# All 32 hidden rows of the MLP down projection by seven products, with half 0's norm rows beneath the last two stages

## The chip, the cores and the metric

One core of a Trainium2 chip runs the whole program. The metric is the time of one execution on the device in microseconds (us): the median of several runs of the kernel before is 2182.65. TensorE multiplies matrices, ScalarE (ACT in the profile) and VectorE (DVE) work on tiles of 128 partitions, SyncE (SP) issues loads, and ScalarE also issues stores.

## The reference

A trunk of two layers over 1024 rows of 1024 features. Layer 0 has a short convolution, layer 1 latent attention whose keys and values are made once from the stream after layer 0. Each layer ends with an MLP of 4096 hidden features. What the change touches is the MLP's second product and the norm and residual behind it:

```python
def squared_relu_mlp(h, w_up, w_down):
    return jnp.square(jax.nn.relu(h @ w_up)) @ w_down
...
        y = squared_relu_mlp(h, mlp_up_w[l], mlp_down_w[l])
        x = x + g_f[:, None, :] * rmsnorm(y, norm_g[l, 3])
```

In layer 0 the new x is normed again (without its gains, which are folded into later scales), turned into columns and multiplied by the latent weights `q_a_w` and `kv_a_w`. In layer 1 it is the output. All of it is in float32.

## The kernel before

Every float32 operand is split into a high and a low part (`split_w`: ScalarE writes the high part, L160, VectorE subtracts it for the low part, L161), and a product is three matmuls, high by low, low by high, high by high (`mm`, L157). A step of the down projection is thus a row of splits that ScalarE and VectorE must have finished, and then matmuls.

The hidden activations are 32 rows of 128 features, in DRAM, transposed: `ha`, seven sums of quarters for pairs of rows, and `hd`, plain rows. `down_pairs` takes 24 of the 32 rows as 12 pairs, and multiplies 2 x 2 blocks in the seven-product way of Strassen and Winograd: seven stages in the order 0, 1, 3, 6, 4, 5, 2, six steps each. A stage accumulates in four PSUM banks, one for each row tile t; a pair of stages that share a result go on in the same banks. A step loads its operand `raw<-ha` through four buffers (`raw_tile`), splits it into a ring buffer `pa` (three of them), splits its quarter of the weight, which stays in its own room `w`, into a ring buffer `pb` (two), and runs 24 matmuls. After a stage, `sums`, `add` or `copy` bring the banks into the eight result tiles `ys`, rows 128 t to 128 t + 127. Half 0 is tiles 0 to 3, half 1 tiles 4 to 7.

`down` then does the other 8 rows directly in chunks of 2, 2 and 4. In its last chunk `Seam.tile` follows for each of the eight row tiles: it adds the last bank, takes squares and root on ScalarE (L246, L248), scales (L303), adds the residual row (L304) and stores it; in layer 0 it takes the squares again, and `flush` writes the normed row into the result tile (L286). `first_block` makes the first three latents of half 0 with the transposes of half 1 between.

The order on each engine is fixed when the program is built: a scheduler moves instructions, but inside `pinned` those of the named engines (SP's alone where none is named) keep the order in which they are written. SP issues loads in order, and where one of them waits for a buffer, all behind it wait. The lines that matter here are few:

```python
    def ld(out_, in_):
        nc.sync.dma_start(out_, in_)
...
                nc.vector.tensor_tensor(xr, xr, y, op=ALU.add)
                nc.scalar.dma_start(self.xdst[t * P:(t + 1) * P, :], xr)
```

## Time and profile before

| | before |
|---|---|
| three runs, us | 2182.33, 2182.65, 2184.46 |
| profiled execution, us | 2181.45 |
| its span, us | 2179.7 |
| granted TensorE clock, mean | 0.992 |
| TensorE, VectorE, ScalarE busy | 96%, 70%, 48% |
| layer 0: products; direct rows; first latents, us | 716 to 955; to 1044; to 1070 |
| layer 1: direct rows to the end, us | 2083 to 2180 |

A row of the timeline has the start, the duration, the engine, the line, the operation and its tiles; in square brackets is the idle time before it and what ended that. TensorE's matmuls overlap, so what counts is the distance between starts. Groups have the count, then busy time and mean nanoseconds, then the idle time before them. Numbers of buffers are left out of names: `ring` is any of the ring buffers, `raw` any buffer of loads.

### The profile page before, as it was taken

The numbers are of one execution on the slowest core, as the hardware profiler recorded it, in microseconds if no ns is written. First come the engines' busy times: TensorE is split into PE (matmuls) and PEld (weight loads), VectorE is DVE, ScalarE is ACT, GpSimd is POOL, SyncE is SP. The second block draws the span as 40 slices with busy tenths as digits, with TensorE's granted clock in tenths as the row PEclk, the third lists the DMA queues.
The fourth block names the chain that finished last, engine by engine and source line by source line (L and its number), as shares of the span: only waits on it lengthen the run. The fifth ranks groups of instructions, "written<-read, shape, count | busy, mean of one in ns | idle before, by whom it ended". The sixth has DMA issues, their size and how long they took to land.

```text
span 2179.7 us, 25250 instructions
## 1 busy us (share of the span) xinstructions
PE 2093.7 (96%) x9638; PEld 1715.7 (79%) x9638; DVE 1530.3 (70%) x2063; ACT 1052.2 (48%) x1501; POOL 4.0 (0%) x8
## 2 busy tenths in 40 slices
PE   4999999899999999999899999999899999999998
PEld 3778888678888788888777888877688887788886
DVE  6777766876665679766788887666866655566665
ACT  4533354744454444343665655565645544444422
POOL 0000000000000000000000000000000000000000
PEclk9999999999999999999999999999999999999999
DMA  7435464256443986554223231053254544842343
GB/s 226 131 119 154 128 203 144 78 164 193 160 159 104 342 292 199 162 168 147 85 66 122 69 113 44 30 185 115 81 164 156 179 160 153 295 174 97 127 134 116
DMA packets 233552, 323.52 MB, mean 148 GB/s; under 512 B 18165, under 2 KB 141394, under 8 KB 233430
## 3 DMA queue, kind: packets, MB, share of 16 engines
q1 hardware_dynamic: 198424, 244.11, 35.7%
q10 hardware_dynamic: 35006, 77.79, 9.3%
q8 instruction: 76, 1.25, 0.2%
q14 instruction: 46, 0.38, 0.1%
HBM read 244.26 MB, written 77.59 MB: 148 GB/s over the span
## 4 chain that ended last, share of the span: by engine, by line
PE 79%; DVE 11%; ACT 6%; issue 2%; DMA 1%; ACTq 0%; SPq 0%; DVEq 0%
PE one L157 39%; PE mm L157 19%; PE big L157 9%; PE tp L157 6%; PE big L1280 2%; ACT junk L246 2%; DVE y L303 2%; DVE raw L304 2%; PE tp L1306 1%; DVE y L297 1%; ACT z L1137 1%; DMA aw<-in_ada_w_dram 1%; ACT small L248 1%; DVE av L823 1%; PE tp L399 0%
## 5 line engine op out<-in xcount | busy, mean ns | idle before, releaser
L157 PE MATMUL one<-slot,uphi 128*128 128x512 f32 x1224 | 378.3, 390 | 0.0
L157 PE MATMUL big<-slot 128*128 128x512 f32 x1536 | 354.3, 391 | 0.6 <-DVE slot L161 0.6
L157 PEld LDWEIGHTS big<-slot 128*128 128x128 f32 x1536 | 288.5, 188 | 60.5 <-DVE slot L161 0.8
L157 PEld LDWEIGHTS one<-slot,uphi 128*128 128x128 f32 x1224 | 230.8, 189 | 48.3 <-issue 0.5
L157 PE MATMUL one<-slot,uplo 128*128 128x512 f32 x612 | 241.0, 394 | 8.1 <-ACT y L565 2.3
L161 DVE TENSOR_TENSOR uplo<-raw,uphi 128x1024 fp32r<-128x1024 f32 x127 | 153.2, 1221 | 131.6 <-ACT uphi L160 131.5
L157 PE MATMUL one<-ring,ring 128*128 128x512 f32 x864 | 198.2, 390 | 2.8 <-DVE ring L161 2.8
L160 ACT ACTIVATE ring<-w 128x1024 fp32r<-128x1024 f32 x84 | 88.9, 1059 | 224.0 <-PE tp L157 117.5
L160 ACT ACTIVATE uphi<-raw 128x1024 fp32r<-128x1024 f32 x127 | 134.5, 1061 | 121.6 <-PE one L157 89.4
L157 PEld LDWEIGHTS one<-ring,ring 128*128 128x128 f32 x864 | 161.7, 188 | 38.3 <-ACT ring L160 3.1
L157 PE MATMUL mm<-slot,uphi 128*128 128x512 f32 x520 | 164.2, 396 | 9.7 <-DVE slot L364 9.3
L161 DVE TENSOR_TENSOR ring<-w,ring 128x1024 fp32r<-128x1024 f32 x84 | 102.7, 1223 | 89.0 <-ACT ring L160 86.7
L157 PEld LDWEIGHTS one<-slot,uplo 128*128 128x128 f32 x612 | 115.4, 189 | 35.7 <-ACT y L490 3.3
L157 PE MATMUL mm<-ring,ring 128*128 128x512 f32 x576 | 139.5, 390 | 0.1
L157 PE MATMUL tp<-ring,ring 128*128 128x512 f32 x576 | 138.7, 389 | 0.0
L187 DVE SCALAR_TENSOR_TENSOR acc<-raw,csil,acc 128x1024 f32<-128x1024 f32 x88 | 112.5, 1279 | 32.3 <-DMA raw<-in_ada_w_dram 29.2
L157 PEld LDWEIGHTS mm<-ring,ring 128*128 128x128 f32 x576 | 107.6, 188 | 23.5 <-issue 0.8
L157 PEld LDWEIGHTS tp<-ring,ring 128*128 128x128 f32 x576 | 108.1, 188 | 22.4
L157 PEld LDWEIGHTS mm<-slot,uphi 128*128 128x128 f32 x520 | 97.2, 189 | 33.2 <-DVE slot L364 10.8
L490 ACT ACTIVATE y<-one 128x512 f32<-128x512 f32 x66 | 39.0, 591 | 165.8 <-PE one L157 95.7
L157 PE MATMUL one<-slot,s 128*128 128x512 f32 x468 | 112.6, 389 | 0.0
L161 DVE TENSOR_TENSOR ring<-raw,ring 128x1024 fp32r<-128x1024 f32 x84 | 102.4, 1219 | 11.9 <-ACT ring L160 11.9
(252 smaller groups left out, 3495.9 us busy)
## 6 DMA issues: line engine op xcount, KB each, us to landing
ha<-y ACTq DMA_DIRECT2D x168, 256.0 KB, 4.0
raw<-ha SPq DMA_DIRECT2D x84, 512.0 KB, 4.3
raw<-in_ada_w_dram SPq DMA_DIRECT2D x80, 512.0 KB, 4.2
raw<-in_mlp_up_w_dram SPq DMA_DIRECT2D x70, 512.0 KB, 4.2
w<-in_mlp_down_w_dram SPq DMA_DIRECT2D x48, 512.0 KB, 6.7
raw<-hd SPq DMA_DIRECT2D x32, 512.0 KB, 4.3
hd<-y ACTq DMA_DIRECT2D x24, 512.0 KB, 3.6
xs<-raw ACTq DMA_DIRECT2D x24, 512.0 KB, 2.9
```

The costliest lines, as they stand in the source:

```text
L157: nc.tensor.matmul(out_, lhs[a], rhs[b], start=first and i == 0, stop=last and i == 2, skip_group_check=more)
L160: nc.scalar.activation(hi, src, AF.Copy)
L161: nc.vector.tensor_tensor(lo, src, hi.bitcast(F32), op=ALU.subtract)
L187: nc.vector.scalar_tensor_tensor(acc, raw, s, acc, op0=ALU.mult, op1=ALU.add)
L246: nc.scalar.activation(junk, src, AF.Square, accum_out=ss)
L248: nc.scalar.activation(rt, ss, AF.Sqrt, bias=eps_d)
L297: nc.vector.tensor_tensor(y, y, p_, op=ALU.add)
L303: nc.vector.scalar_tensor_tensor(y, y, rroot(ss), self.gmb, op0=ALU.mult, op1=ALU.mult)
L304: nc.vector.tensor_tensor(xr, xr, y, op=ALU.add)
L490: nc.scalar.activation(dst, x_, AF.Copy)
L823: nc.vector.scalar_tensor_tensor(acc, raw[:, i, :], csil[:, i:i + 1], acc, op0=ALU.mult, op1=ALU.add)
L1280: nc.tensor.matmul(o_, a, m_, start=j == 0, stop=j == 4)
```

## The change

All 32 rows now go through `down_pairs`, as 16 pairs, eight steps per stage. `down` no longer has a share in the MLP. The rings are four `pa` and three `pb`, with a fourth in the last stage, "2". The weight quarter "21" has no room of its own any more: it is loaded through the four raw buffers, in stage "1" and again in stage "2". In `mlp_up`, the first four pairs of rows make their seven quarter sums too, in place of two plain stores.

Half 0's results are complete after the fifth stage ("4"). Its four norm rows are now run beneath the last two stages, "5" and "2": tiles 0, 1 and 2 at the first, fourth and seventh step of stage "5", tile 3 at the second step of stage "2" (`half0`). Their residual rows go into tiles of their own, `xr` for odd t and `acc` for even t, one buffer each; `early` loads the residual of tile t + 2 behind the step after tile t's row. In layer 0 the transposes and evictions of half 0's columns (`h_steps`, now with two evictions by ScalarE and no VectorE copy) follow from the fourth step of stage "2" on. The last four steps of stage "2" (`LATE`) are taken by row tiles: for each t the matmuls of the four steps, and then the norm row of tile 4 + t. `first_latents` makes the first three latents one after the other, with half 1's transposes in the third. The build also sets the size of a DMA scratch area to 256.

SP's loads in layer 1 at the start of stage "5", before (`ha_110` is that stage's operand):

```order
L115 DMA raw_15651<-ha_110 128x2x512
L115 DMA raw_15682<-ha_110 128x2x512
L115 DMA raw_15713<-ha_110 128x2x512
L115 DMA raw_15744<-ha_110 128x2x512
L115 DMA raw_15775<-ha_110 128x2x512
L115 DMA raw_15806<-ha_110 128x2x512
```

And after, from the same place (`xs_104` holds the residual rows):

```order
L115 DMA xr_16020<-xs_104 128x1024
L115 DMA xr_16022<-xs_104 128x1024
L115 DMA raw_16025<-ha_110 128x2x512
L115 DMA raw_16066<-ha_110 128x2x512
L115 DMA xr_16072<-xs_104 128x1024
L115 DMA raw_16099<-ha_110 128x2x512
L115 DMA raw_16130<-ha_110 128x2x512
L115 DMA raw_16171<-ha_110 128x2x512
L115 DMA xr_16177<-xs_104 128x1024
```

The operands stood one behind the other; now two residual rows stand ahead of the first, a third between the second and the third, a fourth behind the fifth.

ScalarE in layer 0, after, in stage "5" (`y_5364` and `y_5365` are the results of tiles 0 and 1, `xr_6886` tile 0's residual; `w_5403` to `w_5406` are the weights of the second to the fifth step; `ring_5389` serves the second and the fifth):

```order
L160 ACTIVATE ring_5389<-w_5403 128x1024
L246 ACTIVATE junk_6897,small_6898<-y_5364 128x1024
L248 ACTIVATE small_6900<-small_6898,eps_d 128x1
L160 ACTIVATE ring_5385<-w_5404 128x1024
L160 ACTIVATE ring_5387<-w_5405 128x1024
L304 DMA xs_103<-xr_6886 128x1024
L246 ACTIVATE junk_6907,small_6908<-xr_6886 128x1024
L160 ACTIVATE ring_5389<-w_5406 128x1024
L248 ACTIVATE small_6910<-small_6908,eps_d 128x1
L246 ACTIVATE junk_7010,small_7011<-y_5365 128x1024
L286 ACTIVATE y_5364<-xr_6886,small_6943 128x1024
L248 ACTIVATE small_7013<-small_7011,eps_d 128x1
```

The splits stood alone there; the norm of two row tiles now stands among them, and tile 0's last write (L286) behind the split for the fifth step.

ScalarE in layer 0, after, at the end of stage "2" (`h` and `tt` are half 0's columns, `raw` operands and weights of the last steps):

```order
L160 ACTIVATE ring_5386<-raw_7408 128x1024
L398 ACTIVATE h_1001_7210<-one_7379,v_6226,v_5924 128x512
L398 ACTIVATE tt_7384<-one_7379,v_6226,v_5924 128x512
L398 ACTIVATE h_1001_7210<-one_7397,v_6226,v_5924 128x512
L398 ACTIVATE tt_7402<-one_7397,v_6226,v_5924 128x512
L398 ACTIVATE h_1001_7210<-one_7415,v_6226,v_5924 128x512
L398 ACTIVATE tt_7420<-one_7415,v_6226,v_5924 128x512
L160 ACTIVATE ring_5388<-raw_7426 128x1024
L160 ACTIVATE ring_5389<-raw_7423 128x1024
L398 ACTIVATE h_1001_7210<-one_7433,v_6226,v_5924 128x512
L398 ACTIVATE tt_7438<-one_7433,v_6226,v_5924 128x512
L160 ACTIVATE ring_5390<-raw_7444 128x1024
```

Six evictions of transposed columns stand ahead of the splits into `ring_5388` and `ring_5389`, those of the seventh step; two more ahead of the eighth's.

The diff, without the pool layout, the removed `first_block` and the calls of the attention phase:

```diff
-ROWS = 8
 LAG = 2
-PAIRS = (D_FF // P - ROWS) // 2
+PAIRS = D_FF // P // 2
+LATE = 4
...
             y = self.ys[t]
-            if t == 0:
-                self.load(0)
-                self.load(1)
-            self.load(t + 2)
+            for i in range(t, t + self.ahead):
+                self.load(i)
             xr = self.xr[t]
             with pinned():
-                nc.vector.tensor_tensor(y, y, p_, op=ALU.add)
+                if add:
+                    add()
                 self.back()
...
-    def h_steps(tp, ys, half, key, dst):
+    def h_steps(tp, ys, half, key, dst, room=tp_ps, twice=False):
         hi, lo = dst
         s1, sh = vtile["s" + key], vtile["h" + key]
         tts = {}
         def step(k):
-            p_ = tp_ps()
+            p_ = room()
             for t in range(4):
                 nc.tensor.transpose(p_[:, t * P:(t + 1) * P], ys[half * 4 + t][:, k * P:(k + 1) * P], ident)
             tt = tp.tile([P, HALF], F32, tag="tt", name=nm("tt"), bufs=2)
-            nc.scalar.activation(tt, p_, AF.Identity, scale=s1[:, k:k + 1], bias=sh[:, k:k + 1])
+            for out_ in (hi[:, k, :], tt) if twice else (tt,):
+                nc.scalar.activation(out_, p_, AF.Identity, scale=s1[:, k:k + 1], bias=sh[:, k:k + 1])
             tts[k] = tt
         def split(k):
-            nc.vector.tensor_copy(hi[:, k, :], tts[k])
+            if not twice:
+                nc.vector.tensor_copy(hi[:, k, :], tts[k])
             nc.vector.tensor_tensor(lo[:, k, :], tts[k], hi[:, k, :].bitcast(F32), op=ALU.subtract)
...
-                elif k == 1:
-                    seam.back()
-                elif k >= 4:
-                    seam.back()
-                    seam.front(steps1, 2)
+                    if m == 0 and k == 0:
+                        seam.flush()
+                    elif m == 2:
+                        seam.back()
+                        seam.front(steps, 1)
+            ps_.append(p_)
         with pinned():
             seam.back()
         return ps_
...
-    def down_pairs(ys, wd, before):
+    def down_pairs(ys, wd, before, seam, key=None, preps=()):
+        r1, r2, r3, l1 = pool("r1", "right"), pool("r2", "right"), pool("r3", "right"), pool("l1")
         n = PAIRS // 2
-        w4 = wd[ROWS * P:, :].rearrange("(q two p) d -> p q two d", two=2, p=P)
-        sl = pool("sl")
-        ws = [{} for _ in range(n)]
...
+        def room(q, b, order):
+            for i in order:
+                ws[b][i] = q.tile([P, 2, HALF], F32, name=nm("w"))
+        def ring(q):
+            return q.tile([P, 2, 2, HALF], F32R, name=nm("ring"))
+        rings = [ring(r1) for _ in range(7)]
+        room(r2, "22", range(n))
+        room(r3, "11", [5, 6, 7, 0, 1, 2, 3, 4])
+        room(l1, "12", range(n))
+        pas, pbs = rings[0::2], rings[1::2]
         count = 0
-        def get(i, b):
-            ld(ws[i][b], w4[:, 2 * i:2 * i + 2, int(b[0]) - 1, (int(b[1]) - 1) * HALF:int(b[1]) * HALF])
-        def less(i, b, x_, y_):
-            nc.vector.tensor_tensor(ws[i][b], ws[i][x_], ws[i][y_], op=ALU.subtract)
+        steps = []
...
             nc.vector.tensor_tensor(u, u, p_, op=ALU.add)
             for half in range(2):
                 nc.vector.tensor_tensor(spot(half, t, 1), spot(half, t, 1), u, op=ALU.add)
+        def products(p_, t, pa, pb, first, last, more):
+            ts_ = slice(t * P, (t + 1) * P)
+            for q in range(2):
+                mm(p_, (pa[:, 0, q, ts_], pa[:, 1, q, ts_]), (pb[:, 0, q], pb[:, 1, q]), first and q == 0, last and q == 1, more)
+        def early(t):
+            q, tag = (xp, "xr") if t % 2 else (ad, "acc")
+            seam.load(t, q.tile([P, D], F32, tag=tag, name=nm("xr"), bufs=1))
+        def half0(i):
+            if i in (0, 3, 6, n + 1):
+                seam.ahead = 1
+                seam.tile((0, 3, 6, n + 1).index(i), None, [])
+            with pinned():
+                if i in (1, 4, 7, n + 2):
+                    seam.flush()
+                    early((1, 4, 7, n + 2).index(i) + 2)
+                if i > n + 2:
+                    seam.back()
+                    seam.front(steps, 1)
+            if i in (n, n + 2, n + 7) and preps:
+                preps.pop(0)(up)
         with pinned([mybir.EngineType.SP]):
             for which, one, more, b, make, done in (
...
                 if not more:
                     banks_ = [bank_ps() for _ in range(4)] if one else [mm_ps(), mm_ps(), tp_ps(), tp_ps()]
                     spare[0] = mm_ps if one else bank_ps
-                if which == 2:
-                    sl.release()
-                    arb = pool("arB")
-                    first = slots_of(arb, SLOTS - 4)
+                late = []
+                if which == 5:
+                    l1.release()
+                    xp = pool("xp")
+                    early(0)
+                    early(1)
+                elif which == 2:
+                    r3.release()
+                    r4 = pool("r4", "right")
+                    pbs.append(ring(r4))
+                    if key:
+                        h0 = pool("h0")
+                        dst = tuple(h0.tile([P, KD, HALF], F32R, name=nm("h0")) for _ in range(2))
+                        up = pool("up")
+                        steps = h_steps(tp, ys, 0, key, dst, bank_ps, True)
                 for i in range(n):
-                    if which in (0, 1, 3, 6):
-                        get(i, b)
+                    wb = ws[b][i] if b != "21" else raw_tile().rearrange("p (q m) -> p q m", q=2)
+                    if which in (0, 1, 3, 6, 2):
+                        get(wb, i, b)
                     if make == "t3":
-                        less(i, "11", "22", "11")
+                        less(wb, ws["22"][i], wb)
                     elif make:
-                        less(i, b, b, make)
+                        less(wb, wb, ws[make][i])
                     raw = raw_tile().rearrange("p (q m) -> p q m", q=2)
                     ld(raw, ha[which][2 * i:2 * i + 2].rearrange("q p m -> p q m"))
-                    pa, pb = pas[count % 3], pbs[count % 2]
+                    m = len(pbs)
+                    pa, pb = pas[count % 4], pbs[i % 4 if m == 4 else count % 3]
                     count += 1
                     with pinned([mybir.EngineType.Activation, mybir.EngineType.DVE]) if before else nullcontext():
                         split_w(pa[:, 0], pa[:, 1], raw)
-                        split_w(pb[:, 0], pb[:, 1], ws[i][b])
+                        split_w(pb[:, 0], pb[:, 1], wb)
                         if before:
                             before.pop()()
-                    if which == 2 and i >= n - 2:
-                        fill_row(first[i - n + 2], wd, from_dram(hd), i - n + 2)
-                    if which:
+                    if which not in (0, 5, 2):
                         run_bg(1 + (i % 3 == 0))
+                    if which == 5:
+                        half0(i)
+                    if which == 2 and i >= n - LATE:
+                        half0(n + i)
+                        late.append((pa, pb))
+                        continue
                     for t in range(4):
-                        ts_ = slice(t * P, (t + 1) * P)
-                        for q in range(2):
-                            mm(banks_[t], (pa[:, 0, q, ts_], pa[:, 1, q, ts_]), (pb[:, 0, q], pb[:, 1, q]),
-                               i == 0 and q == 0 and not more, i == n - 1 and q == 1, more)
+                        products(banks_[t], t, pa, pb, i == 0 and not more, i == n - 1, more)
                         if i == n - 1:
                             done(t, banks_[t])
-        run_bg(99)
+                    if which == 2:
+                        half0(n + i)
+                if which == 4:
+                    run_bg(99)
+            seam.ahead = 4
+            for t in range(4):
+                with pinned([mybir.EngineType.PE]):
+                    for j, (pa, pb) in enumerate(late):
+                        products(banks_[t], t, pa, pb, False, j == LATE - 1, True)
+                    seam.tile(4 + t, lambda: done(t, banks_[t]), [])
+                    with pinned():
+                        seam.front(steps, 1)
         spare[0] = mm_ps
-        sd.release()
-        ara = pool("arA", "right")
-        return [ara, arb, pool("arC")], first + slots_of(ara, 4)[::-1]
-    def down(slots, sizes, wd, src_fn, ys, seam, steps, per_chunk_bg, before_last=None, begun=False):
+        for q in (r4, r2, r1):
+            q.release()
+        if not key:
+            xp.release()
+        if key:
+            return xp, h0, dst, up
+    def down(slots, sizes, wd, src_fn, ys, seam, steps, per_chunk_bg, before_last=None):
         f = 0
...
-            if 2 * i < ROWS:
-                for f, t_ in enumerate((a, b)):
-                    nc.scalar.dma_start(hd[2 * i + f], t_)
-            else:
-                late.append(lambda: sums(i - ROWS // 2, *halves(a), *halves(b)))
+            late.append(lambda: sums(i, *halves(a), *halves(b)))
...
-    ar, slots = down_pairs(ys, mlp_down_w[0], last)
+    ws = []
+    seam = Seam(nx, ys, vtile["g0f"], xs[0], xs[1])
+    xp, h0, hq0, up = down_pairs(ys, mlp_down_w[0], last, seam, "1m",
+                             [lambda up, i=i: ws.append(up_weights(up, [q_a_w[0][:, i * P:(i + 1) * P]])) for i in range(3)])
     banks(False)
-    up, ws, hs, firsts, ys = down_phase(slots, (2, 2, 4), mlp_down_w[0], from_dram(hd), "g0f", xs[0], xs[1], q_a_w[0], "1m", ys=ys,
-                                       pairs=False)
-
```

More of the change, by code (lines that the diff above doesn't have):

```diff
@@ L265, in __init__, with load @@
             self.nx, self.ys, self.gmb, self.xsrc, self.xdst, self.last = nx, ys, gmb, xsrc, xdst, last
-            self.rest, self.backs, self.xr = None, [], {}
-        def load(self, t):
-            if t < NT:
-                self.xr[t] = raw_tile()
+            self.rest, self.backs, self.xr, self.ahead = None, [], {}, 3
+        def load(self, t, room=None):
+            if t < NT and t not in self.xr:
+                self.xr[t] = room or raw_tile()
                 ld(self.xr[t], self.xsrc[t * P:(t + 1) * P, :])
@@ L324, in as_quarter @@
         return [(slot[:, kk, :HALF], slot[:, kk, HALF:]) for kk in range(4)]
-    def as_h(slots, pair):
-        return tuple(slots[i].rearrange("p a (b m) -> p (a b) m", b=2) for i in pair)
     def quarter_steps(ys, key, ops):
@@ L728, in down @@
                 slot = slots[f % SLOTS]
-                if f >= 2 or not begun:
-                    fill_row(slot, wd, src_fn, f)
+                fill_row(slot, wd, src_fn, f)
                 rows.append(slot)
@@ L743, in down @@
                 if f == nf:
-                    seam.tile(t, p_, steps)
-                elif f == n_rows and not begun:
+                    seam.tile(t, lambda: nc.vector.tensor_tensor(ys[t], ys[t], p_, op=ALU.add), steps)
+                elif f == n_rows:
                     nc.scalar.activation(ys[t], p_, AF.Copy)
@@ L1001, in trunk_kernel, with down_phase @@
     conv_phase()
-    def down_phase(slots, sizes, wd, src_fn, g, xsrc, xdst, next_w, key, ys=None, pairs=True):
-        begun = ys is not None
-        ys = ys or [row_tile() for _ in range(NT)]
+    def down_phase(slots, sizes, wd, src_fn, g, xsrc, xdst, next_w, key):
+        ys = [row_tile() for _ in range(NT)]
         up = pool("up", "right")
@@ L1437, in trunk_kernel @@
     ys = [row_tile() for _ in range(NT)]
[L1438 to L1442 removed]
+    down_pairs(ys, mlp_down_w[1], last, Seam(nx, ys, vtile["g1f"], xs[2], out[0], last=True))
     for q in (tp, nx, yp, ad, rawp, cp, wide[0], ps, dr):
```

99 lines of the change are left out of this document (37 added, 62 removed).

## The prediction

> **What bounds the kernel now.** I read the page first, then the waits of TensorE in the two stretches that change, then its timeline there. The page:
>
> ```profile
> span 2179.7 us, 25250 instructions
> PE 2093.7 (96%) x9638; PEld 1715.7 (79%) x9638; DVE 1530.3 (70%) x2063; ACT 1052.2 (48%) x1501; POOL 4.0 (0%) x8
> PE 79%; DVE 11%; ACT 6%; issue 2%; DMA 1%; ACTq 0%; SPq 0%; DVEq 0%
> ```
>
> The profiled run took 2181.45 us, 1.8 around the span and 1.2 under the median of the three runs, 2182.65. TensorE is 79% of the chain that ends last. Its waits in 690 to 1160 us (layer 0: products, the eight rows done directly, first latents), then in 1830 to 2180 us (layer 1):
>
> ```profile
> PE tp L399 <- ACT tt L401: 3.6, 2, 2.6
> PE one L157 <- DVE ring L161: 1.7, 2, 1.1
> ...
> PE one L157 <- DVE ring L161: 1.1, 1, 1.1
> ```
>
> So the product stages wait 1.7 and 1.1 us in all: they are bound by TensorE, at a pitch that the timeline gives:
>
> ```profile
> 2077.85 2.88 PE L157 MATMUL mm<-ring,ring 128*128 128x512 f32 x12
> 2080.57 2.88 PE L157 MATMUL tp<-ring,ring 128*128 128x512 f32 x12
> 2083.29 87.20 PE L157 MATMUL big<-slot 128*128 128x512 f32 x384
> ```
>
> Twelve matmuls start every 2.72 us, 0.227 us each. A step of a product is four row tiles of six matmuls, 24 in 5.44 us. The last row is the direct part in layer 1: 384 matmuls.
>
> **What is saved.** Four more pairs by products cost two more steps in each of seven stages, 7 x 2 x 24 = 336 matmuls, in place of 384. That is 48 x 0.227 = 10.9 us per layer. Two smaller gains. In layer 0 two gaps before the first latents go, since half 0's transposes move earlier:
>
> ```profile
> 1045.21 1.33 PE L399 MATMUL tp<-cs,y 128*128 128x128 f32 x8 [0.98 <-ACT tt L401]
> ...
> 1051.24 1.33 PE L399 MATMUL tp<-cs,y 128*128 128x128 f32 x8 [2.62 <-ACT tt L401]
> ```
>
> 3.6 us. In layer 1 the add at the very end shrinks from 1024 to 512 columns:
>
> ```profile
> 2170.53 1.22 DVE L297 TENSOR_TENSOR y<-y,big 128x1024 f32<-128x1024 f32 x1
> ...
> 2176.07 0.34 ACTq L305 DMA_DIRECT2D out_dram<-raw  x1
> ```
>
> At 512 columns an add takes 0.68 (row at 891 us below), so 0.5 is saved. With nothing against it the change gives 10.9 + 3.6 + 10.9 + 0.5 = 25.9 us, to 2155.5 in the profiled run's time.
>
> **What is added off the path.** The first four pairs now make seven quarter sums and 256 KB stores each, for two 512 KB stores: 16 subtractions of 512 columns per layer, 16 x 0.68 = 11 us of VectorE under some 270 us of up projection, where it is 70% busy. I take 0 (bounds 0 and 2 per layer); without TensorE's cover it would be the 11. The stores land long before the stage that loads them. The order of the conv phase is nearly as it was, ±2, taken as 0.
>
> **What waits: the norm rows' residual loads.** Half 0's rows now need their residual in the two tiles `xr` and `acc`. The load of tile t+2 must wait until tile t is through with the same buffer, and it is issued on SP, in order, ahead of the next step's operand `raw<-ha`. SP does block on such waits today, but far ahead of need:
>
> ```profile
> SPq L115 <- DVE ring L161: 111.7, 38, 13.1
> SPq L115 <- DMA xs<-raw: 45.9, 6, 21.3
> ```
>
> Columns: total, times, longest. Now the lead is used up: the load behind the wait is that of the step two ahead. Durations, from the groups of 690 to 1160 us and the landings there (the last two in layer 1):
>
> ```profile
> L161 DVE TENSOR_TENSOR ring<-raw,ring 128x1024 fp32r<-128x1024 f32 x42 | 51.2, 1219 | 6.6 <-ACT ring L160 6.6
> L160 ACT ACTIVATE ring<-w 128x1024 fp32r<-128x1024 f32 x42 | 44.5, 1059 | 115.4 <-PE tp L157 58.7 <-PE one L157 46.2 <-issue 10.4
> L303 DVE SCALAR_TENSOR_TENSOR y<-y,small,gmb 128x1024 f32<-128x1024 f32 x8 | 10.3, 1285 | 0.3
> L304 DVE TENSOR_TENSOR raw<-raw,y 128x1024 f32<-128x1024 f32 x8 | 9.8, 1225 | 0.3
> L286 ACT ACTIVATE y<-raw,small 128x1024 f32<-128x1024 f32 x8 | 9.1, 1141 | 0.2
> L246 ACT ACTIVATE junk<-y 128x1024 bf16<-128x1024 f32 x8 | 8.4, 1044 | 17.3 <-DVE y L297 17.3
> L248 ACT ACTIVATE small<-small,eps_d 128x1 f32<-128x1 f32 x16 | 4.7, 295 | 0.5
> raw<-ha SPq DMA_DIRECT2D x39, 512.0 KB, 4.9
> ...
> w<-in_mlp_down_w_dram SPq DMA_DIRECT2D x20, 512.0 KB, 7.0
> ...
> raw<-ha SPq DMA_DIRECT2D x42, 512.0 KB, 3.9
> out_dram<-raw ACTq DMA_DIRECT2D x8, 512.0 KB, 2.6
> ```
>
> The sums at the end of the stage before (`sums`, L667 and L669) outlast TensorE:
>
> ```profile
> 884.65 1.28 DVE L667 TENSOR_TENSOR y<-y,one 128x512 f32<-128x512 f32 x2
> ...
> 891.25 0.68 DVE L669 TENSOR_TENSOR y<-y 128x512 f32<-128x512 f32 x1
> 887.56 1.75 PE L157 MATMUL mm<-ring,ring 128*128 128x512 f32 x7
> ```
>
> TensorE is in the next stage at 887.56, the last sum ends at 891.9, 4.4 us later. Let R = 0 be that start; a step ends every 5.44.
>
> *Third step of stage "5", layer 1.* SP's load of tile 2's residual waits for the landing of tile 0's output store. That store waits for the row's add, which stands on VectorE behind the split of the fourth step's weight, whose buffer TensorE frees at 5.44: 5.44 + 1.06 + 1.22 + 1.23 = 8.9, landed at 11.5, two issues of about 0.35 each later (the last store's issue takes 0.34, row above) the operand is under way, lands after 3.9 to 4.9 beside the residual, say at 16.6, split by 1.05 + 1.22 at 18.9. TensorE wanted it at 10.88: **8.0 us** (7.5 to 10).
>
> *The same in layer 0.* Here the row is also normed: the load waits for the ScalarE write L286, and ahead of that in ScalarE's order stands the split of the fifth step's weight, which waits for TensorE's second step, 10.88. So 10.88 + 1.06 + 0.30 + 1.04 + 1.14 = 14.4, two issues, landing 4.9, split 2.3: 22.3, **11.4 us** late (10 to 12.5). This one closes on itself: the load for the third step cannot leave before the second has ended.
>
> *Fourth step of stage "2".* Tile 3's row stands behind the splits of the third step, whose operand is loaded only when the first step's buffer is free, 1.6 before the stage starts; landed 2.9, split 4.0, root and squares, then five VectorE operations of 1.2: its add ends near 9.1, the store lands at 11.7. Then residual, weight and operand, three loads: 17.2 at 4.4, the weight's subtraction, two splits, 21.8 against 16.3: **5.5** (0 to 7). In layer 0 another load and the norm's second pass stand in the same place: **8** with 2 at the second step (5 to 11 in all, I take **10**).
>
> *The last four steps.* They run by row tiles, so the last of the four operands is wanted 4 us after the first, not 16. In layer 1 weight and operand now share four raw buffers, and the eighth step's pair is loaded when the sixth's is split: about 38 against 31.3, **6** (0 to 7). In layer 0 ScalarE's evictions of three transposed columns, which wait for transposes that stand on TensorE behind the fourth step, are ahead of the splits of the seventh and eighth steps: 3.5 + 2.2 + 0.6 by the same rows; the first latents then wait for the row tiles of half 1. Together **8** (0 to 12).
>
> *Stage "1" of layer 0* pulls its weights, its operands and 1.33 background loads per step through the four raw buffers, 3.33 in all. A buffer is held for a landing and two splits, 4.9 + 2.3 = 7.2; 7.2 / 4 x 3.33 = 6.0 per step of 5.44, 4.4 over eight steps, of which the lead of the ring buffers covers about half: **2** (0; or 9 where landings take 5.6, still under the weights' 7.0 above).
>
> **The clock.** What an idle TensorE costs behind the wait is in this trace, at 435 us. Timeline, then windows (start:end length, busy of PE, PEld, DVE, ACT, POOL, granted clock, DMA share, GB/s):
>
> ```profile
> 438.38 1.00 PE L157 MATMUL mm<-slot,uphi 128*128 128x512 f32 x2 [3.25 <-DVE slot L364]
> ...
> 440.00:442.00 2.00, 2.00 (x6) 1.58 (x5) 1.43 (x4) 0.65 (x2) 0.00 (x0) 0.50 0.73 203
> 442.00:444.00 2.00, 2.00 (x10) 1.58 (x10) 1.58 (x3) 1.04 (x1) 0.00 (x0) 0.98 1.00 351
> ```
>
> After 3.25 us of waiting the clock is 0.50 for some 4 us, half of them lost: 2 us per long wait. The 2.62 us wait above kept 1.00. The Trainium skill, "TensorE: Matmul & The Clock Gate" (HAM clock gate), says as much: half clock after an idle window of about 3.4 us, and as long again to recover; this trace agrees. I count 2 us for the two waits in stage "5" and the one in stage "2" of layer 0, 6 in all; in layer 1 the later start of the last steps swallows it.
>
> **Sum.** Layer 0: -10.9 - 3.6 + 2 + 11.4 + 10 + 8 + 4 = +20.9. Layer 1: -10.9 - 0.5 + 8.0 + 5.5 + 6 + 2 = +10.1. Together +31 on 2181.45 gives 2212.5; with 1.2 to the median, 2213.7. I state **2212**, 1.3% slower.
>
> **Rivals.** *The saving comes through* (chance 0.14): the loads land in time and the rows hide beneath the products; 2155.5 + 1.2, about 2157, to 2172 with half of the stage "5" waits. For it: SP waits of 13.1 and 21.3 us cost TensorE nothing before. The Trainium skill, "DMA: Bandwidth & Descriptors" (Issuing engines are not separate DMA queues), gives the reason one would have: which engine issues a transfer matters only for the time to initiate it. By that the load's place is worth one issue, 0.34 us. Against it: those old waits guarded buffers whose contents were wanted later. It decides if the third step's operand lands by 10.88 - 2.3 = 8.6, so if tile 2's load leaves by 3.7, before the sums that its buffer's row needs have ended at 4.4. I keep the chance for a wait that I have read wrongly in the order.
>
> *Only stage "5" stalls* (0.12): the lead of later loads covers stage "2" and the end; -25.9 + 8.0 + 11.4 + 4 = -2.5, 2180, within 0.2% or a little faster. For it: the bounds of those terms reach 0.
>
> *The four raw buffers become the bound* (0.12): stage "1" of layer 0 costs 9, and the last four steps 12 and 7; 2213.7 + 7 + 4 + 1 = 2226. It decides once landings reach 5.6; the weights of today, 7.0, speak for it, the operands, 3.9 and 4.9, against.
>
> *The change does less than it says* is as good as excluded: on TensorE the order has 336 for 384 in each layer.
>
> The forecast itself, stalls in both stages, has 0.62. A measurement of this kernel tells 0.2%, 4.4 us, from no change. **Range** 2180 to 2230: all low ends of the terms together take 28 off, to 2186, all high ends add 18, to 2231; the second rival draws it down to 2180, and the first is left out. Faster 0.17, same 0.07, slower 0.76.
>
> **What would show it.** In the changed kernel's waits, TensorE at the products should wait for ring splits by 40 to 60 us in all, in four to six waits of 5 to 12 us; the longest should be layer 0's third step of stage "5", with SP waiting for ACT there and for the output's store in layer 1; the granted clock should dip behind each. If instead the product stages run at 2.72 us per twelve with waits under 3 us, I am wrong, and the time lies near 2157. If stage "5" alone waits, the sum's later terms were wrong.

## The result and the profile after

The changed kernel takes 2223.14 us, the median of five runs (2221.93 to 2228.04), against 2182.65 before: 1.0186 times as long, 95% interval 1.0172 to 1.0200. It lost 40.5 us. The forecast was 2212 us, slower, with a range of 2180 to 2230.

The page of the changed kernel:

```profile
span 2226.0 us, 25233 instructions
PE 2090.2 (94%) x9542; PEld 1707.9 (77%) x9542; DVE 1536.3 (69%) x2079; ACT 1084.3 (49%) x1533; POOL 4.0 (0%) x8
PE 76%; DVE 11%; ACT 6%; DMA 4%; issue 2%; SPq 0%; ACTq 0%; DVEq 0%
```

TensorE has 96 instructions less, as the change says, and is 94% busy where it was 96%. DMA was 1% of the chain that ends last and is 4%. Its waits in layer 0 (690 to 1160 us), then in layer 1 (1830 us to the end):

```profile
PE mm L157 <- DVE ring L161: 26.5, 7, 11.0
PE big L157 <- ACT tt L398: 6.1, 1, 6.1
...
PE mm L157 <- DVE ring L161: 18.4, 5, 9.0
```

Waits for ring splits came to 1.7 and 1.1 us before. Now the two last stages add 26.5 and 18.4, and the first latent waits another 6.1.

Where the 46.3 us between the two profiled spans lie, by the starts of the same work in the two timelines (the first product of `down_pairs`, TensorE's first sum over the squares of the latents):

| stretch | before | after | difference | forecast |
|---|---|---|---|---|
| start to layer 0's products | 716.4 | 714.1 | -2.3 | 0 |
| to that sum over the latents' squares | 357.8 | 382.9 | +25.1 | +20.9 |
| attention, to layer 1's products | 778.4 | 786.0 | +7.6 | 0 |
| layer 1's products to the end | 327.1 | 343.0 | +15.9 | +10.1 |

The changed kernel's profiled execution, 2228.04 us, is its slowest run, 4.9 above the median. A kernel of the experiments that differs from it only in the side on which two pools lie, with a span of 2219.9, has -1.6, +24.6, +6.6 and +10.6 in these rows. So most of what the profiled run has beyond the median lies in its last row. The four rows of that other trace add up to 40.2, close to the 40.5 between the medians; it is called the trace near the median below.

The third step of stage "5" in layer 0, all engines in order of time (start, duration):

```profile
951.83 1.06 ACT L160 ACTIVATE ring<-w 128x1024 fp32r<-128x1024 f32 x1 [0.43 <-PE tp L157]
...
954.25 1.15 ACT L286 ACTIVATE y<-xr,small 128x1024 f32<-128x1024 f32 x1
...
955.42 0.33 SPq L115 DMA_DIRECT2D xr<-xs  x1
...
955.80 1.45 SPq L115 DMA_DIRECT2D raw<-ha  x3
...
960.37 1.06 ACT L160 ACTIVATE ring<-raw 128x1024 fp32r<-128x1024 f32 x1 [0.47 <-DMA raw<-ha]
...
962.74 3.78 PE L157 MATMUL mm<-ring,ring 128*128 128x512 f32 x8 [10.95 <-DVE ring L161]
```

The stage began at 940.75. ScalarE's split for the fifth step waits for TensorE's second step; behind it L286 writes tile 0's normed row until 955.40; SP, held until then, issues the residual at 955.42 and the third step's operand right behind. That lands about 960.3, when ScalarE's wait for it ends, and TensorE starts at 962.74, 22.0 after the stage's start and after 10.95 of idle time. In layer 1 the row is not normed, and the store holds SP:

```profile
2110.06 1.22 DVE L303 TENSOR_TENSOR xr<-xr,y 128x1024 f32<-128x1024 f32 x1
...
2111.31 0.34 ACTq L304 DMA_DIRECT2D out_dram<-xr  x1
...
2114.02 0.33 SPq L115 DMA_DIRECT2D xr<-xs  x1
2114.45 1.67 SPq L115 DMA_DIRECT2D raw<-ha  x3
...
2122.26 2.08 PE L157 MATMUL mm<-ring,ring 128*128 128x512 f32 x4 [9.04 <-DVE ring L161]
```

The store was issued at 2111.31 and landed 2.7 later, and SP goes on. The fourth step of stage "2" in layer 0 has the same form, with tile 3's row in the place of tile 0's:

```profile
1013.40 1.15 ACT L286 ACTIVATE y<-xr,small 128x1024 f32<-128x1024 f32 x1 [0.23 <-DVE small L253]
1014.58 0.34 SPq L115 DMA_DIRECT2D xr<-xs  x1
...
1016.12 0.41 SPq L115 DMA_DIRECT2D raw<-ha  x1
...
1026.88 3.54 PE L157 MATMUL mm<-ring,ring 128*128 128x512 f32 x7 [10.93 <-DVE ring L161]
```

Behind each of these waits the granted clock falls to half. After the first of them (windows: start, end and length, then PE, PEld, DVE, ACT and POOL busy, the clock, DMA share and GB/s):

```profile
962.00:964.00 2.00, 1.26 (x3) 1.07 (x4) 0.76 (x2) 1.04 (x2) 0.00 (x0) 0.50 0.91 338
964.00:966.00 2.00, 2.00 (x6) 1.52 (x6) 1.23 (x1) 1.53 (x3) 0.00 (x0) 0.50 0.45 182
966.00:968.00 2.00, 2.00 (x8) 1.59 (x7) 1.23 (x1) 0.58 (x1) 0.00 (x0) 0.71 0.40 143
```

And the first latent of layer 0:

```profile
1071.09 0.77 ACT L398 ACTIVATE tt<-one,v,v 128x512 f32<-128x512 f32 x1
...
1071.91 0.79 PE L157 MATMUL big<-h,uplo 128*128 128x512 f32 x1 [6.10 <-ACT tt L398]
```

Its first matmul starts when ScalarE has read the last transposed column out of its bank.

### The profile page after: what moved, and what is told of

Same layout as the page of the kernel before. It is cut to its first block, busy times and chain, and to the rows that moved or that the text cites. A ratio compares the mean times of both kernels' runs of the same rounds, so it can differ in the third digit from the quotient of the medians.

```text
span 2226.0 us, 25233 instructions
## 1 busy us (share of the span) xinstructions
PE 2090.2 (94%) x9542; PEld 1707.9 (77%) x9542; DVE 1536.3 (69%) x2079; ACT 1084.3 (49%) x1533; POOL 4.0 (0%) x8
## 4 chain that ended last, share of the span: by engine, by line
PE 76%; DVE 11%; ACT 6%; DMA 4%; issue 2%; SPq 0%; ACTq 0%; DVEq 0%
PE one L157 41%; PE mm L157 19%; PE tp L157 6%; PE big L157 4%; PE big L1313 2%; ACT junk L246 2%; DMA raw<-ha 1%; DVE y L302 1%; PE tp L1339 1%; DVE ring L161 1%; DMA raw<-in_mlp_down_w_dram 1%; DVE raw L303 1%; DMA aw<-in_ada_w_dram 1%; ACT z L1170 1%; ACT ring L160 1%
## 5 line engine op out<-in xcount | busy, mean ns | idle before, releaser
L157 PE MATMUL one<-ring,ring 128*128 128x512 f32 x1152 | 263.3, 390 | 2.3 <-DVE ring L161 2.3
L157 PEld LDWEIGHTS one<-ring,ring 128*128 128x128 f32 x1152 | 215.8, 188 | 48.3 <-ACT ring L160 3.1
L157 PE MATMUL mm<-ring,ring 128*128 128x512 f32 x768 | 199.6, 411 | 45.3 <-DVE ring L161 44.9
L160 ACT ACTIVATE ring<-raw 128x1024 fp32r<-128x1024 f32 x144 | 149.5, 1053 | 164.6 <-DMA raw<-ha 97.1
L161 DVE TENSOR_TENSOR ring<-raw,ring 128x1024 fp32r<-128x1024 f32 x144 | 174.4, 1221 | 79.0 <-ACT ring L160 78.5
L157 PEld LDWEIGHTS mm<-ring,ring 128*128 128x128 f32 x768 | 151.4, 199 | 83.0 <-DVE ring L161 33.8
L157 PE MATMUL tp<-ring,ring 128*128 128x512 f32 x768 | 184.3, 390 | 0.0
L157 PE MATMUL big<-slot 128*128 128x512 f32 x768 | 179.9, 395 | 4.6 <-DVE slot L161 4.5
L157 PEld LDWEIGHTS big<-slot 128*128 128x128 f32 x768 | 145.6, 190 | 35.8 <-DVE slot L161 5.2
L157 PE MATMUL mm<-slot,uphi 128*128 128x512 f32 x344 | 108.6, 397 | 9.5 <-DVE slot L360 9.3
```

Source lines behind the costliest of these rows:

```text
L157: nc.tensor.matmul(out_, lhs[a], rhs[b], start=first and i == 0, stop=last and i == 2, skip_group_check=more)
L160: nc.scalar.activation(hi, src, AF.Copy)
L161: nc.vector.tensor_tensor(lo, src, hi.bitcast(F32), op=ALU.subtract)
```

## The experiments

Two theories to begin with. Q: a residual load waits for a norm row, and SP, whose loads go out in the order in which they are written, keeps the next operand behind it. L: loads and the four raw buffers are too slow for a step of 5.44 us, whatever the order. Kernels are compared with the kernel before, on the same chip; the ratio's interval is of 95%.

**Tile 2's residual load moved.** In `half0` the load stands behind the fifth step of stage "5", not the second:

```diff
-                if i in (1, 4, 7, n + 2):
-                    seam.flush()
-                    early((1, 4, 7, n + 2).index(i) + 2)
+                if i in (1, 4, 7, n + 2):
+                    seam.flush()
+                if i in (4, 4, 7, n + 2):
+                    for t in [t for t, at in zip((2, 3, 4, 5), (4, 4, 7, n + 2)) if at == i]:
+                        early(t)
```

> Tile 2's residual load is moved on SP from behind the second step of stage "5" to behind the fifth; nothing else changes. Theory Q (the load waits for tile 0's row, and SP keeps the third step's operand behind it): the waits of 11.0 (layer 0) and 9.0 us (layer 1) at that step vanish, and with each some 2 us at half clock, -24 us, so about 2199 us (2194 to 2205); the 11.1 and 6.5 us waits in stage "2" stay. Theory L (the landings or the four raw buffers are too slow for a step of 5.44 us, whatever the order): the wait only moves to a later step, 2215 to 2225.

Measured: 2202.06 us, 1.0088 (1.0072 to 1.0105). That is 21 us off by the place of one load per layer, 3 less than expected: both waits at the third step are gone, but in layer 0 a new one of 6.3 stands at the sixth step. The waits at the fourth step of stage "2", which were to stay, have shrunk with the earlier start, from 10.9 and 6.3 to 5.8 and 5.2. Waits of this kernel, layer 0 and layer 1:

```profile
PE mm L157 <- DVE ring L161: 15.5, 6, 6.3
...
PE mm L157 <- DVE ring L161: 8.1, 5, 5.2
```

**The load in its place, with a buffer of its own.** What holds it is taken away, not its place on SP:

```diff
-            q, tag = (xp, "xr") if t % 2 else (ad, "acc")
+            q, tag = (xq, "xq") if t == 2 else (xp, "xr") if t % 2 else (ad, "acc")
...
                     xp = pool("xp")
+                    xq = pool("xq")
```

> Tile 2's residual load stays where it stands on SP, but goes into a buffer of its own, so that it waits for no row. Theory Q: its wait was the cause, not its place, so the two waits at the third step of stage "5" vanish all the same, 2199 us (2194 to 2205), within 4 us of the kernel with the load moved. Theory P (an additional transfer of 512 KB at that place delays the operand by its own time): the waits shrink but 2 to 5 us remain in each layer, 2203 to 2212.

Measured: 2197.53 us, 1.0069 (1.0050 to 1.0088). Waits of this kernel, layer 0 and layer 1:

```profile
PE mm L157 <- DVE ring L161: 12.0, 3, 6.3
...
PE mm L157 <- DVE ring L161: 6.7, 5, 3.3
```

The two waits at the third step are gone here too, though SP issues the same loads in the same order, so it was the wait for the buffer and not the additional 512 KB ahead of the operand (theory P). The Trainium skill, "DMA: Bandwidth & Descriptors" (Issuing engines are not separate DMA queues), says that initiating transfers on several engines saves only the sequencer's time to initiate, usually small beside the transfer itself. Here an issue takes 0.33 us; the 9 to 11 us were the wait in front of it. The 6.3 us wait at the sixth step of layer 0 stands here as well.

**Tile 5's load moved too**, from behind the third step of stage "2" to behind the seventh (`(4, 4, 7, n + 6)` in the same place):

> As with tile 2's load moved, and tile 5's load too, from behind the third step of stage "2" to behind the seventh. Theory Q: the waits of 11.1 and 6.5 us at the fourth step vanish with their half clock, another -21 us; the last four steps, whose start comes earlier, give 2 to 4 us back in layer 1. About 2179 us (2172 to 2186). Theory L: stage "2" loads weights and operands through four buffers and stays behind by 4 to 8 us per layer, 2187 to 2196.

Measured: 2186.8 us, 1.0016 (1.0006 to 1.0025). Another 15.3 us off, not 21. The waits at the fourth step of stage "2" are gone in both layers, and layer 1 keeps 3.1 us in all. The expectation had taken these waits from the changed kernel, 11.1 and 6.5; with tile 2's load moved only 5.8 and 5.2 were left to win. It had also left out the 6.3 us at the sixth step of stage "5", which both kernels have. Tile 3's load, behind the fifth step, waits for tile 1's norm in the same way, as the next kernel shows.

**All four loads moved**: `(4, 7, n + 3, n + 6)`.

> As the kernel with tile 2's and tile 5's loads moved (2186.8 us), and the loads of tiles 3 and 4 moved as well, tile 3's from behind the fifth step of stage "5" to behind the eighth, tile 4's to the fourth of stage "2". In layer 0 a wait of 6.3 us at the sixth step of stage "5" remained there. Theory Q: tile 3's load waits for tile 1's norm and holds the sixth step's operand; the wait vanishes with its half clock, 2178 us (2174 to 2183). Theory L (four raw buffers): it stays or moves on, 2184 to 2188.

Measured: 2175.28 us, 0.9962 (0.9947 to 0.9976): faster than before. Waits of layer 0, then of layer 1:

```profile
PE big L157 <- ACT tt L398: 5.8, 1, 5.8
PE one L395 <- ACT tt L398: 3.1, 1, 3.1
...
PE mm L157 <- DVE ring L161: 1.1, 2, 0.6
...
PE mm L157 <- DVE ring L161: 1.9, 2, 1.3
```

From 26.5 and 18.4 us of waits for ring splits, 1.1 and 1.9 are left. The computation, its buffers and its transfers are those of the changed kernel; in the source only the places of four loads on SP differ. Theory L predicted 2184 to 2188 and falls. 48 us of the changed kernel's time hung on the places of four loads on one queue. With the loads the scheduler also moved some splits on ScalarE and VectorE ahead of norm rows, in and near these two stages (33 of ScalarE's 1533 instructions and 64 of VectorE's 2079 stand elsewhere in the order); what that alone is worth, no run separates.

**Rows of layer 1 not beneath the stages.** In layer 1 alone, half 0's four norm rows go into the loop at the end, one beside each of half 1's, with their residual loads (`if not key: return` in `half0`, `early(t)` ahead of each row tile, and in the loop):

```diff
+                    if not key:
+                        seam.tile(t, None, [])
                     seam.tile(4 + t, lambda: done(t, banks_[t]), [])
```

> The changed kernel, but in layer 1 half 0's four norm rows are not beneath stages "5" and "2": each goes into the loop at the end, beside that of half 1. Theory Q: all of layer 1's waits in the stages vanish (9.0 + 6.5 us, some 4 in the last steps, 2 + 2 at half clock), and the end grows, since a tile's two rows take VectorE some 5.9 us against TensorE's 5.44, by 3 to 7 us: 2223.1 - 23 + 5 = 2205 us (2199 to 2210). Theory B (rows beneath are worth their stalls): the end grows by four whole rows' chains, 4 x 5 us, 2218 to 2226.

Measured: 2212.32 us, 1.0124 (1.0107 to 1.0141), 10.8 faster than the changed kernel, not 18, so between the two theories. All waits in layer 1's stages are gone (1.1 us left, as before the change), but the end was mis-sized. Its end, in the timeline:

```profile
2193.22 0.68 DVE L655 TENSOR_TENSOR y<-y,tp 128x512 f32<-128x512 f32 x1
...
2202.77 0.68 DVE L655 TENSOR_TENSOR y<-y,tp 128x512 f32<-128x512 f32 x1
...
2206.52 1.23 DVE L303 TENSOR_TENSOR raw<-raw,y 128x1024 f32<-128x1024 f32 x1
```

(The first two lines are the adds of tiles 6 and 7, the last is the last sum with a residual.) The norm rows run one behind the other, 9.55 us for a tile's two, 2193.22 to 2202.77, since VectorE waits for ScalarE's squares and root within each; I had counted VectorE's work alone, 5.9. TensorE's last matmul starts near 2189.5, and the end comes 22 us later; in the changed kernel 9.1. By these two ends, rows beneath the stages are worth 13 us, if they cost nothing there.

**Transposed columns in the last loop.** On the kernel with tile 2's and 5's loads moved, all eight columns of half 0 go into the loop over row tiles, two ahead of each norm row (the call in `half0` goes, which is not printed here):

```diff
+                    with pinned():
+                        seam.front(steps, 2)
                     seam.tile(4 + t, lambda: done(t, banks_[t]), [])
-                    with pinned():
-                        seam.front(steps, 1)
```

> Both loads moved as before, and in layer 0 all eight transposed columns of half 0 go into the loop over row tiles, two behind each tile's matmuls and ahead of its norm row. If ScalarE's evictions ahead of the last steps' splits (4.6 us of waits) and those behind the last norm row (6.3 us and 2 at half clock) are what the end of layer 0 costs, 8 to 12 us go: 2169 us (2163 to 2176). If the row tiles' chain of half 1 sets that end, less than 4 us go: 2176 to 2182.

Measured: 2191.2 us, 1.0038 (1.0023 to 1.0052), 4.4 slower than without, a miss. The latents now wait longer, on the same operation:

```profile
PE big L157 <- ACT tt L398: 9.5, 1, 9.5
```

That the first matmul, which reads the first column, should wait for the last one gave the next theory, K: the bank is wanted, not the column. `banks(False)` ahead of the latents gives the wide banks (`big`) out of the memory in which the columns were transposed.

**Another bank for the first latent**, on the kernel with all four loads moved:

```diff
-            p_ = mm_ps() if m else big_ps()[:, :HALF]
+            p_ = mm_ps() if m < 2 else big_ps()[:, :HALF]
```

> The kernel with all four residual loads moved (2175.3 us), and the first of the three latents in a bank of its own kind (mm) in place of one of the wide pair (big), which is given out only when the banks of the transposed columns are read. Theory K (the wait of 5.8 us at the start of the latents is for those banks, not for the columns: its first matmul needs the first column, done long before): the wait vanishes with 2 us at half clock, 2167.5 us (2164 to 2171). Theory H (the last columns are late): the wait moves to the last matmuls of that latent, 2171 to 2176.

Measured: 2168.25 us, 0.9937 (0.9921 to 0.9954). K holds: the wait is gone, and what remains for splits, columns and banks in the two layers' products is

```profile
PE one L395 <- ACT tt L398: 3.1, 1, 3.1
...
PE mm L157 <- DVE ring L161: 1.2, 3, 0.6
...
PE mm L157 <- DVE ring L161: 3.0, 2, 2.4
```

It is the fastest of all kernels here, 14 us faster than the kernel before.

**Four attempts at the rest.** (1) On the fastest kernel: one transposed column beneath the fourth step of stage "2", then three, two and two in the loop:

> As before, and half 0's transposed columns go one beneath the fourth step of stage "2" and then three, two, two into the first three row tiles of the last loop, ahead of the norm row, in place of five in a row behind that step. If the wait of 3.1 us of the fifth for a free bank is a cost of its own, it goes: 2164 us (2160 to 2168). If ScalarE's evictions in the loop (1.55 us for a column beside 5 us for a norm row, against 5.44) hold the rows up in its place, nothing is won: 2167 to 2173.

2177.93 us, 0.9980 (0.9971 to 0.9989), slower than either expectation, by 9.7 us against the fastest: the 3.1 us are gone, and in their place stand

```profile
PE mm L157 <- DVE ring L161: 6.0, 4, 2.3
PE tp L395 <- ACT y L286: 4.8, 1, 4.8
```

The last norm rows of half 1 come later, and the transposes of the third latent wait for them. (2) On the same kernel: the columns begun a step earlier, four in a row (`if n + 1 < i < n + 7`):

> The fastest so far (2168.3 us), with half 0's transposed columns begun one step earlier, beneath the third step of stage "2", so that four and not five stand in a row behind the fourth. Theory N (four banks: the fifth in a row waits 3.1 us for a bank): that wait goes, 2165.5 us (2163 to 2168). If it is ScalarE's order (evictions behind the splits of the last steps), the fourth waits in its place, 2167 to 2170; if tile 3's norm row is not done by the third step, 2170 to 2175.

2175.2 us, 0.9963 (0.9951 to 0.9975), 7 us slower. The fifth column's wait for a bank goes, as theory N has it, and one for a split comes:

```profile
PE mm L157 <- ACT ring L160: 5.2, 1, 5.2
```

My reading is that ScalarE, with two evictions of 0.77 for each column, is what the end of layer 0 has too little of; no run tests it by taking evictions away. (3) On the changed kernel: all four rows in stage "5", with residual buffers of their own, four columns in the first steps of stage "2" and four in the loop, and attention's pools placed as in (4). The line for the rows, of several:

```diff
-            if i in (0, 3, 6, n + 1):
+            if i in (0, 2, 4, 6):
```

> Products for all 32 rows, with half 0's four rows all in stage "5" (first, third, fifth, seventh step), residual rows in buffers of their own that wait for no row, the first four transposed columns in the first steps of stage "2" and the other four in the first two row tiles of the last loop, and attention's pools on the right. Theory Q: no wait over 3 us is left in layer 1's stages and at most one of 3 to 5 at layer 0's end; 2186.8 - 8 - 10 - 5 = 2164 us (2157 to 2173), faster than the kernel before. Theory L: 2175 to 2190.

2178.76 us, 0.9982 (0.9972 to 0.9992), in the range of theory L and not in that of Q. Yet layer 1's stages wait no more than 2.0 us in all, as Q has it. Layer 0 keeps 3.7 us at the third latent's transposes, and the first step of stage "2" there waits 5.5 us, on VectorE's order:

```profile
985.19 0.69 DVE L655 TENSOR_TENSOR y<-y,tp 128x512 f32<-128x512 f32 x1 [0.67 <-PE tp L157]
985.79 1.22 DVE L646 TENSOR_TENSOR raw<-raw,w 128x1024 f32<-128x1024 f32 x1
987.11 2.00 ACT L160 ACTIVATE ring<-raw 128x1024 fp32r<-128x1024 f32 x2 [2.69 <-DVE raw L646]
...
990.61 5.20 PE L157 MATMUL mm<-ring,ring 128*128 128x512 f32 x12 [5.46 <-DVE ring L161]
```

The subtraction for that step's weight (L646) now stands on VectorE behind the last adds of stage "5" (L655), which wait for TensorE, and ScalarE waits 2.69 us for it before it can split; in the changed kernel it stood ahead of them. (4) Attention's pools on the other side of the memory, in the changed kernel (`pool("tb", "right")`, `pool("at", "right")`):

> The changed kernel, with attention's work pools on the right side of the memory, so that the first two slots of the output projection's weights lie on memory that is free during attention. If the wait of 4.5 us at the start of that projection is for the release of those pools, it falls to 0 to 1 us, 2223.1 - 4 to 7 = 2218 us (2215 to 2220). If it is a late load or the transposes' chain, nothing changes, 2222 to 2225.

2221.77 us, 1.0174 (1.0159 to 1.0190): nothing moved. The wait it was aimed at is a new one of the changed kernel, at the start of attention's output projection:

```profile
1394.79 0.33 SPq L115 DMA_DIRECT2D raw<-hd  x1
...
1455.53 0.33 ACTq L1375 DMA_DIRECT2D hd<-o  x1
...
1455.90 3.90 ACT L160 ACTIVATE slot<-raw 128x1024 fp32r<-128x1024 f32 x4 [0.40 <-ACT o L1374]
...
1459.40 15.91 PE L157 MATMUL big<-slot 128*128 128x512 f32 x56 [4.54 <-DVE slot L161]
```

The load shown was issued 61 us ahead of the splits. They stand on ScalarE behind attention's last store; before, they stood ahead of its last two, at 1424.63. Whether the scheduler puts them there for their memory is open; a kernel with the slots filled early was not tried.

## Why the prediction was right, and where it was off

The direction, its cause and the place of each long wait in the two stages held. The sum, +31 on the profiled execution, was 9 short by the trace near the median, 15 by the changed kernel's own.

- **What is saved.** 48 matmuls per layer less, and the end in layer 1 shorter by 0.5 (9.6 to 9.1 us from the last matmul's start): as predicted. The two gaps of 3.6 us ahead of layer 0's latents are gone too, but the latents' new wait, below, is longer than they were.
- **Third step of stage "5".** Layer 0: 11.4 predicted, 10.95 measured, SP released at 14.67 after the stage's start where the sum had 14.4. Layer 1: 8.0 and 9.04; the store was issued at 9.1 (8.9) and landed after 2.7, and the operands took longer. The two experiments on tile 2's load show the cause.
- **Fourth step of stage "2".** Layer 0: 10 for two steps; 10.93 at the fourth and 1.3 in smaller waits ahead of it. Layer 1: 5.5 and 6.31.
- **The last four steps.** Layer 0: 8; the splits' waits there are 3.3 (2.19, 0.57 and 0.57) and the latents' 6.1, together 9.4. That the sum is near is luck: 6.3 of the 8 were counted for the splits and 1.7 for the latents, and the reason given for these, rows of half 1, was wrong: it was the bank. Layer 1: 6 predicted, 3.1 measured, and 3.1 again in the kernel with tile 2's and 5's loads moved, where the fourth step does not wait. The term was too large.
- **Stage "1" of layer 0.** 2 predicted (0 to 9), 0 measured. The rival of the four raw buffers, 2226 us, ends near the measured time, but for another reason, and the moved loads contradict it.
- **The clock: mis-sized.** 6 us were counted, 2 for each of three waits. By the distances of matmuls that started 0.33 to 0.48 apart, against 0.227, while nothing was waited for, 5.7 us were lost in layer 0's stretch and 7.2 in layer 1's, against 0.5 each before: 12. In the trace near the median it is 6.3 and 3.9, so 9. All long waits had it, the latents' and layer 1's fourth step too, which the count left out. Layer 1's last steps had it in the profiled execution, not in the trace near the median, and the clock is 3.3 of the 5.3 us by which the former's last row is longer.
- **Attention and the up projections: not priced.** I had read the order only for the parts that the diff names. The output projection waits 4.5 us where it waited 0.6 and had nine of its matmuls done beforehand. The up projections, from TensorE's first wait for L490's addition to the products, are 2.0 us longer in layer 0 and 2.7 in layer 1 (2.0 and 2.2 in the trace near the median), at my upper bound of 2 or above it, not 0; the new sums (L1081 to L1084) stand on VectorE ahead of an addition that TensorE waits for:

```profile
461.02 0.68 DVE L1084 TENSOR_TENSOR y<-y,y 128x512 f32<-128x512 f32 x1
...
462.95 0.68 DVE L490 TENSOR_TENSOR y<-y,one 128x512 f32<-128x512 f32 x1
...
463.68 0.50 PE L157 MATMUL one<-slot,uplo 128*128 128x512 f32 x1 [1.13 <-DVE y L490]
```

The row from attention to layer 1's products is 6.6 to 7.6 us longer, and these two are most of it: the largest piece of what the sum lacked. The conv phase, taken as 0 within 2, gained some 4 (the first row of the table without layer 0's up projection); why, no run shows.
- **The rival that the saving comes through** named its own condition, that tile 2's load leave by 3.7 us into the stage. It left at 14.67 and 11.83. Where the loads are moved and the first latent has another bank, that rival comes nearly true: 2168, against 2157 for it; the 11 us between lie mostly in the attention's start, the up projections and the waits left at layer 0's end.

One sentence of the description of the kernel was wrong: `pinned` without names keeps the order on every engine except SP, and SP's is kept by the `pinned` around all stages of `down_pairs`. No step of the prediction rests on it.

## What to carry to other kernels

A load that must wait for a buffer belongs on its queue behind everything that is wanted before that buffer can come free: give it the last place from which it still lands in time, or a buffer of its own. Price such a wait from the release back (what stands on each engine ahead of the instruction that frees the buffer), and where the released instruction itself stands behind a wait for the stage's own progress, expect idle time of more than a step (here 9.0 to 11.0 us at a step of 5.44), with half a clock behind it. When a change rearranges memory or adds work elsewhere, read the order of the untouched phases too: here the largest piece of what the sum lacked lay in attention and the up projection behind it, which the diff hardly names.

## What the hardware showed that was not expected

The clock does not go by the longest single wait. In layer 1's last steps of the changed kernel's profiled execution no wait is longer than 2 us, and it fell to half all the same:

```profile
2195.66 0.52 PE L157 MATMUL mm<-ring,ring 128*128 128x512 f32 x1 [1.98 <-DVE ring L161]
2196.71 3.78 PE L157 MATMUL mm<-ring,ring 128*128 128x512 f32 x8 [0.52 <-DVE ring L161]
...
2194.00:2196.00 2.00, 0.34 (x1) 0.19 (x1) 1.71 (x2) 1.21 (x2) 0.00 (x0) 0.99 0.84 252
2196.00:2198.00 2.00, 1.48 (x4) 1.10 (x4) 0.65 (x1) 0.00 (x0) 0.00 (x0) 0.50 0.16 66
2200.00:2202.00 2.00, 2.00 (x7) 1.52 (x6) 0.49 (x2) 1.41 (x3) 0.00 (x0) 0.50 0.04 8
```

It was 0.50 from 2196 to 2202, behind waits of 0.57, 1.98 and 0.52. In layer 0, waits of 2.19, 0.57, 0.42 and 0.57 us at 1040 to 1047 left it at 1.00, and so did 0.19, 0.58, 1.11 and 0.57 at the same last steps of layer 1 in the trace near the median. The traces also show a grid: in the changed kernel's, the changes of the granted clock lie at whole multiples of 3.413 us from the first one (2, 5, 118, 120, 272 and so on, to 642), and so they do in all the other kernels' traces. That fits a count over fixed windows, in which similar waits can fall on one side of an edge or the other. The Trainium skill, "TensorE: Matmul & The Clock Gate" (Part 1), describes a free-running window of activity in place of a longest wait; the grid agrees with it. How busy a window must be, no run here measures.
